# Mixer of a two-layer encoder: the Fourier and value projections as one seven-part product, with the mirrored half made by a permutation

## The chip, the core and the metric

The kernel runs on one core of one Trainium2 chip. The metric is the device time of one execution in microseconds (us), median over runs. In the text PE is the matrix engine (TensorE), DVE the vector engine, ACT the scalar engine, POOL GpSimd, and SP the engine that issues most of the transfers. PSUM, where products land, has eight banks; one 128x512 f32 block fills a bank.

## What is computed

Two layers on 512 tokens by 1024 channels. Each layer is a half-step SwiGLU feed-forward block (FFN), a mixer, and a second FFN:

```python
x = x + 0.5 * swiglu(rms_norm(x, ffn1_norm[l]), ffn1_w_in[l], ffn1_w_out[l])
x = x + mixer(rms_norm(x, mix_norm[l]), mix_w_in[l], ...)
x = x + 0.5 * swiglu(rms_norm(x, ffn2_norm[l]), ffn2_w_in[l], ffn2_w_out[l])

def mixer(h, w_in, gate_bias, rpb, w_na_out, w_f_out, w_o):
    z = h @ w_in                      # columns: q 512, k 512, v 512, u 512, two gates of 1024
    y_na = neighbourhood_attention(q, k, v, rpb) @ w_na_out     # 8 heads of 64
    y_f = fourier_mix(u) @ w_f_out    # real part of a 2-D DFT over positions and 128 channels, 4 groups
    g_na, g_f = sigmoid(ga + gate_bias[0]), sigmoid(gf + gate_bias[1])
    return (g_na * y_na + g_f * y_f) @ w_o
```

## The kernel before, in words

**Precision.** Each f32 operand is split into a rounded part and the rest (hi and lo: `split`, L296 to L302; one ACT copy, one DVE subtraction). A product is three matmuls: hi by hi, hi by lo, lo by hi (`mm3` L291, or `late_low` L449, which puts the products with the low half of the weights last). Every weight granule (128x1024 f32, 512 KB) is loaded by SP (L150), rounded by ACT into `whi` (L181) and subtracted by DVE into `wlo` (L184); with `dma=True` or a `plus` key, POOL issues a second transfer that adds another granule in memory (L152). `whi` and `wlo` have three buffers each, so a granule is prepared when the PE has done with the granule three earlier. `Stream` (L255) holds the granules in one fixed order, loads up to 8 ahead and prepares 2 ahead.

**Seven-part products.** The FFN blocks and the gates multiply a 2x2 block matrix in seven block products instead of eight (`ORDER`, `product` L458). A product is 24 matmuls of 512 columns: 4 blocks of 128 input channels, 2 blocks of 128 tokens, 3 matmuls. The left factors of products 4 to 7 are sums and differences of quarters of the activations (t1 to t4), made on DVE from f32 copies `raw` and then split (`combine`, L576, in the FFN); `snap` (L519, ACT) and `less` (L525, DVE) take results out of PSUM.

**Norm.** `quad(i, j)` (L359) transposes one quarter of x on the PE (8 transposes) and writes the split activations. Three quarters are done at the end of the FFN stage (L840, L841, L844) and the last, (1, 0), inside the next stage (`settle`). In the FFN an f32 copy `raw` is kept; in the mixer (`self.mix`) it is not, and each 128x256 piece is split straight out of PSUM (L374). `rstd` (L424) makes the inverse norms with twelve small DVE instructions (L310 to L315, L428, L429); `spread` (L441) sends them through memory into a row `R`, by two POOL transfers.

**Mixer before the change**, in program order (L1315 to L1350):

- `proj_U` (L982): u is wanted as the sum and the difference of token t and token 511-t, for t below 256. It multiplies the first 256 tokens (`straight`) and the last 256 in reversed order (`mirrored`, whose left factor `flip` is a reversed copy made by ACT and DVE, L993 and L994): 96 matmuls.
- `proj_V` (L1027): 96 matmuls. Its results are split into `v` straight out of PSUM.
- `bias_for(0)`: position biases; 68 KB gathers on SP (L1100) into `bw` (2 buffers), then six POOL additions (L1106) into `bm` (4 buffers).
- `four_pos` four times (the transform over positions), `proj_q(0)`, `proj_k(0)` (each 24 matmuls, `proj_T` L970), `four_ch` four times (over channels; each takes two banks, emptied by ACT at L1070 and DVE at L1072 to L1074), `proj_q(1)`.
- Attention by head pairs (L1342): `att_next(hp)` transposes the probabilities of the last pair and starts the scores of the next (four banks); `att_probs` (L1129) does softmax, with eight DVE and sixteen ACT instructions for one pair of heads; `att_outs` multiplies by v.

The instructions of each engine run in the order that a list scheduler gives them when the kernel is built; each engine takes them strictly in that order.

Of the kernel before, what the change touches and what calls it, by code (L numbers as in the profile page):

```python
# [17 lines left out]
P = 128  # L18
# [28 lines left out]
def _granules():  # L47
# [7 lines left out]
    for l in range(L):  # L55
        for w in (1, 2):
# [15 lines left out]
            if w == 1:  # L72
                s = (l, 0)
                for name, n in (("u", 4), ("v", 4), ("qk", 8), ("f", 4)):
                    for g in range(n):
                        put(s, name, g)
                for i in range(2):
                    for g in range(2):
                        put(s, "n", i, g)
                    for q in "acdb":  # L80
                        for g in range(2):
                            put(s, "g" + q, i, g)
                for q in "acdb":
                    for g in range(2):
                        put(s, "w" + q, 0, g)
# [7 lines left out]
def encoder_kernel(  # L93
# [95 lines left out]
    def stage_items():  # L189
# [4 lines left out]

        def strassen(s, name, idx, sizes, order, dma=False):
            def key(q, g):
# [6 lines left out]
            for m in order:  # L203
                for g in range(len(sizes)):
# [7 lines left out]
                    elif m == 4:  # L212
                        add(d2[g])
                    elif m == 5:
                        add(d)
                    elif m == 6:
                        add(d, a, then=b.key if dma else None)
                    else:
                        add(c)

        def out_sizes(c):
# [14 lines left out]
        for l in range(L):  # L236
# [3 lines left out]
            two = (1024, 1024)  # L240
            for name, n in (("u", 4), ("v", 4), ("qk", 8), ("f", 4)):
                for g in range(n):
                    add(Raw((s, name, g)))
            st += 1
# [73 lines left out]
    class Norm:  # L318
# [40 lines left out]
        def quad(self, i, j):  # L359
            self.tiles(i)  # L360
            js = slice(j * 256, (j + 1) * 256)
            hq, lq = self.h[i][:, :, js], self.l[i][:, :, js]
            if not self.mix:
                raw = self.raw[i, j] = slot(F32, "xr")
            for k2 in range(2):
# [5 lines left out]
                for k in range(2):  # L371
                    kt = 2 * k2 + k
                    if self.mix:
                        split(hq[:, kt, :], lq[:, kt, :], tr[:, k, :], self.gain(4 * i + kt))  # L374
                    else:
                        S.activation(raw[:, kt, :], tr[:, k, :], AF.Copy, scale=self.gain(4 * i + kt))
            if not self.mix:
                split(hq, lq, raw)

# [145 lines left out]
    def less(ps, t):  # L525
        for b in range(2):
            V.tensor_tensor(t[:, b, :], ps[b], t[:, b, :], ALU.subtract)  # L527

    def stage_ffn(norm, nxt, late):
# [26 lines left out]
        first = norm.idx == 0  # L556
        norm.tiles(1)
        t4 = (hx[0][:, :, 256:512], lx[0][:, :, 256:512])
# [14 lines left out]

        acts = {1: (hx[0], lx[0], 0), 2: (hx[1], lx[1], 0), 3: (hx[1], lx[1], 256), 4: (*t4, 0)}

        def combine(m):  # L576

            if m == 5:
                V.tensor_tensor(raw[0, 0], raw[0, 0], raw[0, 1], ALU.subtract)
                acts[5] = parts(raw[0, 0], "t1")  # L580
            elif m == 7:
                V.tensor_tensor(raw[0, 1], raw[0, 1], raw[1, 1], ALU.subtract)
                acts[7] = parts(raw[0, 1], "t3")
            elif m == 6:
                V.tensor_tensor(raw[0, 0], raw[1, 1], raw[0, 0], ALU.add)
                acts[6] = parts(raw[0, 0], "t2")
            else:
                V.tensor_tensor(raw[1, 0], raw[1, 0], raw[0, 0], ALU.subtract)
                split(*t4, raw[1, 0])

# [345 lines left out]
    def stage_mixer(l, norm, nxt):  # L936
# [4 lines left out]

        msk = mp.tile([P, 3, 256], F32, tag="msk", name=nm("msk"), bufs=1)
        ch = mp.tile([P, 2, 2, P], F32R, tag="ch", name=nm("ch"), bufs=1)
        R = mp.tile([P, T], F32, tag="R", name=nm("R"), bufs=1)
# [17 lines left out]

        def wide():

            wh, wl = ws.next()
            for k in range(2):
                c = slice(k * T, (k + 1) * T)
                yield wh[:, c], wl[:, c]

        def proj_T(scale):  # L970
            ps = bank()
            wh, wl = ws.next()
            for kt in range(DT):
                c = slice(kt * P, (kt + 1) * P)
                mm3(ps, wh[:, c], wl[:, c], *xs[kt], kt == 0, kt == DT - 1)
            t = tmp(s="q")
            V.tensor_tensor(t, ps, R, ALU.mult)
            hi, lo = hilo("q")
            split(hi, lo, t, scale)
            return hi, lo  # L980

        def proj_U():  # L982
            pss = [bank() for _ in range(4)]

            def straight(kt, wh, wl):
                for c in range(2):
                    lh, ll = [z[:, c * P : (c + 1) * P] for z in xs[kt]]
                    mm3(pss[c], lh, ll, wh, wl, kt == 0, kt == DT - 1)

            def mirrored(kt, wh, wl):  # L990
                flip = tmp(F32R, s="flip")
                xh, xl = [z.bitcast(F32) for z in xs[kt]]
                S.activation(flip[:, 0:256], xh[:, 511:255:-1], AF.Copy)  # L993
                V.tensor_copy(flip[:, 256:512], xl[:, 511:255:-1])  # L994
                for c in range(2):
                    lh, ll = [flip[:, z + c * P : z + c * P + P] for z in (0, 256)]
                    mm3(pss[2 + c], lh, ll, wh, wl, kt == 0, kt == DT - 1)

            for g in range(2):
                for k, w in enumerate(wide()):  # L1000
                    straight(2 * g + k, *w)
                    mirrored(2 * g + k, *w)
                if g == 0:
                    norm.settle()
            w = [*wide(), *wide()]
            for kt in range(4):
                mirrored(4 + kt, *w[kt])
            for kt in range(4):
                straight(4 + kt, *w[kt])
            norm.rstd()  # L1010
            norm.spread(R)
            constants()
            outs = []
            for c in range(2):
                t = tmp(s="uf")
                S.activation(t, pss[2 + c], AF.Copy, scale=norm.rflip[:, c : c + 1])
                both = []
                for op in (ALU.add, ALU.subtract):
                    w = tmp(s="ue")
                    V.scalar_tensor_tensor(w, pss[c], norm.r[:, c : c + 1], t, ALU.mult, op)  # L1020
                    hi, lo = hilo("u")
                    split(hi, lo, w)
                    both.append((hi, lo))
                outs.append(both)
            return outs

        def proj_V():  # L1027
            pss = [bank() for _ in range(4)]
            for g in range(4):
                for k, (wh, wl) in enumerate(wide()):  # L1030
                    kt = 2 * g + k
                    for c in range(4):
                        lh, ll = [z[:, c * P : (c + 1) * P] for z in xs[kt]]
                        mm3(pss[c], lh, ll, wh, wl, kt == 0, kt == DT - 1)
            outs = []
            for c in range(4):
                t = slot(F32R, "v", (2, T))
                split(t[:, 0, :], t[:, 1, :], pss[c], norm.r[:, c : c + 1])
                outs.append(t)
            return outs  # L1040

# [43 lines left out]
        def proj_q(hp):  # L1085
            q[hp] = proj_T(DH**-0.5)

        def proj_k(hp):
            k[hp] = proj_T(None)
            o.append(hilo("o"))  # L1090

# [94 lines left out]

        def att_outs(hp):
            for i in (2 * hp, 2 * hp + 1):
                att_out(i, pt_.pop(i))
# [124 lines left out]

        u = proj_U()  # L1315
        vt = proj_V()
        bias_for(0)
# [6 lines left out]
        vch = {i: (t[:, 0, :], t[:, 1, :]) for i, t in ((0, vt[0]), (1, vs[0]), (2, vt[1]), (3, vs[1]), (4, vt[2]), (5, vs[2]), (6, vt[3]))}  # L1324
        for g in range(4):
            four_pos(g)
        proj_q(0)
        proj_k(0)
        for g in range(4):
            four_ch(g)  # L1330
        proj_q(1)
        def f_rows():
# [8 lines left out]

        for hp in range(3):  # L1342
            att_next(hp)
            bias_for(hp + 1)
            proj_k(hp + 1)
            if hp:
                att_outs(hp - 1)
            if hp < 2:
                proj_q(hp + 2)
        f_some(2)  # L1350


# [18 lines left out]
        swap_pools(0)  # L1371
        f_some(2)
        next(first)
        att_outs(3)
        t12, _ = next(first)
        ws.prep(ws.pos + 2)
        f_some(1)
        bias = []
# [163 lines left out]
def _weights(g):  # L1542
    wst = np.zeros((len(GRAN), P, 1024), np.float32)
    for l in range(L):
# [27 lines left out]
        for i, z in enumerate(_qk_granules(wi)):  # L1572
            wst[GRAN_AT[s, "qk", i]] = z
        for name, m in (("u", u), ("v", v)):
            for i in range(4):
                wst[GRAN_AT[s, name, i]] = _wide(m, (2 * i, 2 * i + 1), 0)

        def four(name, i, w1, c1, w2, c2):
# [4 lines left out]

        wo = g["mix_w_o"][l]
        four("w", 0, wo, 0, wo, T)
        for i in range(2):
# [72 lines left out]
```

## Time and profile before

| | |
|---|---|
| median of 3 runs (lowest, highest) | 1907.44 us (1906.4, 1908.48) |
| the profiled execution, its own time | 1906.98 us |
| its span in the profile | 1905.2 us |
| PE busy | 1890.9 us (99%), 9189 matmuls and transposes |
| DVE, ACT, POOL busy | 1608.4 (84%), 1161.3 (61%), 199.0 us (10%) |
| first mixer, u begins / v begins / four_pos begins | about 336.4 / 359.2 / 381.0 us |
| second mixer, u begins | about 1281.4 us |

How to read it: a matmul's row shows how long it was in the array (389 ns for 512 columns), but the next one starts before it is through, so the distance between two starts is what one costs. A line of the timeline gives the start, the duration, the engine, the source line, the operation, what it writes and reads, its shape and how many such follow each other, and in brackets how long the engine was idle before it and what ended that.

### The profile page before, as it was taken

What the parts mean: (1) busy time and instruction counts of PE and PEld (TensorE: products, weight loads), DVE (VectorE), ACT (ScalarE), POOL (GpSimd) and SP (SyncE); (2) the same over time, 40 slices, a digit from 0 to 9 for tenths busy, and PEclk for the clock granted to TensorE, in tenths of its full rate; (3) what the DMA queues carried; (4) which work ended last, traced back from release to release, by engine and by line L of the source; (5) the groups of instructions that cost most, each with busy time, mean ns of one, the idle gap of its engine ahead of it and who ended that gap; (6) DMA issues with size and microseconds to landing.
All of it is one profiled execution on the core that took longest, in us unless ns stands there. A gap on an engine that the chain in (4) does not pass through costs nothing.

```text
span 1905.2 us, 25187 instructions
## 1 busy us (share of the span) xinstructions
PE 1890.9 (99%) x9189; PEld 1586.3 (83%) x9189; DVE 1608.4 (84%) x2000; ACT 1161.3 (61%) x1676; POOL 199.0 (10%) x246
## 2 busy tenths in 40 slices
PE   9999999999999999999999999999999999999998
PEld 7888888888888888888888888888888888888886
DVE  7877899586889987889997778995769899787898
ACT  6655665467566755566665556663675566555664
POOL 0101010310111011001010100103101101000010
PEclk9999999999999999999999999999999999999999
DMA  9777499323786777649877765974147867776594
GB/s 301 204 209 184 150 254 313 100 73 99 212 217 163 174 199 205 175 154 263 245 189 212 185 178 156 277 266 129 50 121 215 211 172 173 208 177 177 171 276 144
DMA packets 104924, 361.09 MB, mean 190 GB/s; under 512 B 12064, under 2 KB 14240, under 8 KB 104800
## 3 DMA queue, kind: packets, MB, share of 16 engines
q1 hardware_dynamic: 77856, 267.42, 40.4%
q0 software_dynamic: 26800, 92.04, 27.1%
q8 instruction: 72, 1.18, 0.3%
q14 instruction: 52, 0.43, 0.1%
q10 hardware_dynamic: 144, 0.02, 0.0%
HBM read 354.18 MB, written 2.11 MB: 187 GB/s over the span
## 4 chain that ended last, share of the span: by engine, by line
PE 95%; DVE 2%; DMA 1%; ACT 1%; issue 0%; SPq 0%; DVEq 0%; ACTq 0%
PE A L453 9%; PE A L454 9%; PE A L456 9%; PE o L454 7%; PE o L453 7%; PE o L456 7%; PE ps L292 5%; PE ps L293 5%; PE ps L294 5%; PE B L453 5%; PE B L454 5%; PE B L456 5%; PE C L454 2%; PE C L453 2%; PE C L456 2%; PE tr L545 2%
## 5 line engine op out<-in xcount | busy, mean ns | idle before, releaser
L181 ACT ACTIVATE whi<-raw 128x1024 fp32r<-128x1024 f32 (+1 forms) x528 | 546.3, 1037 | 416.9 <-PE A L454 119.2
L184 DVE TENSOR_TENSOR wlo<-raw,whi 128x1024 fp32r<-128x1024 f32 (+1 forms) x528 | 630.1, 1198 | 187.3 <-ACT whi L181 185.2
L152 POOL DMA_DIRECT2D raw<-in_wst_dram x158 | 136.1, 871 | 1283.1 <-DMA raw<-in_wst_dram 631.1
L166 DVE TENSOR_TENSOR raw<-raw,raw 128x1024 f32<-128x1024 f32 (+1 forms) x146 | 172.2, 1189 | 1.2
L454 PE MATMUL A<-whi,xl 128*128 128x512 f32 x384 | 149.5, 389 | 0.0
L453 PE MATMUL A<-whi,xh 128*128 128x512 f32 x384 | 149.4, 389 | 0.0
L456 PE MATMUL A<-wlo,xh 128*128 128x512 f32 x384 | 110.5, 389 | 0.0
L176 ACT ACTIVATE whi<-raw 128x1024 fp32r<-128x1024 f32 (+1 forms) x79 | 81.8, 1035 | 36.2 <-PE A L454 9.6
L177 DVE SCALAR_TENSOR_TENSOR wlo<-raw,whi 128x1024 fp32r<-128x1024 f32 (+1 forms) x79 | 93.2, 1191 | 10.7 <-ACT whi L176 10.6
L638 ACT ACTIVATE th<-sn,rh 128x512 f32<-128x512 f32 x80 | 56.7, 714 | 69.5 <-DVE sn L527 69.5
L522 ACT ACTIVATE sn<-A 128x512 f32<-128x512 f32 x96 | 56.5, 589 | 53.5 <-PE A L456 53.5
L456 PEld LDWEIGHTS A<-wlo,xh 128*128 128x128 f32 x384 | 72.1, 188 | 15.0
L454 PEld LDWEIGHTS A<-whi,xl 128*128 128x128 f32 x384 | 72.1, 188 | 14.8
L453 PEld LDWEIGHTS A<-whi,xh 128*128 128x128 f32 x384 | 72.1, 188 | 14.8
L453 PE MATMUL B<-whi,t1h 128*128 128x512 f32 x192 | 76.2, 397 | 0.0
L453 PE MATMUL A<-whi,t3h 128*128 128x512 f32 x192 | 75.2, 392 | 0.0
L453 PE MATMUL C<-whi,xh 128*128 128x512 f32 x192 | 74.9, 390 | 0.0
L453 PE MATMUL A<-whi,t2h 128*128 128x512 f32 x192 | 74.9, 390 | 0.0
L454 PE MATMUL B<-whi,t1l 128*128 128x512 f32 x192 | 74.8, 390 | 0.0
L454 PE MATMUL A<-whi,t3l 128*128 128x512 f32 x192 | 74.8, 390 | 0.0
L454 PE MATMUL C<-whi,xl 128*128 128x512 f32 x192 | 74.7, 389 | 0.0
L454 PE MATMUL A<-whi,t2l 128*128 128x512 f32 x192 | 74.7, 389 | 0.0
(410 smaller groups left out, 4784.6 us busy)
## 6 DMA issues: line engine op xcount, KB each, us to landing
raw<-in_wst_dram SPq DMA_DIRECT2D x466, 512.0 KB
raw<-in_wst_dram POOLq DMA_DIRECT2D x162, 512.0 KB, 7.8
raw<-in_wst_dram SPq DMA_DIRECT2D x30, 256.0 KB
vs<-v SPq DMA_DIRECT2D x12, 256.0 KB
bw<-in_rpb_dram SPq DMA_DIRECT2D x32, 68.0 KB
x<-in_xin_dram SPq DMA_DIRECT2D x4, 512.0 KB
raw<-in_wst_dram POOLq DMA_DIRECT2D x8, 256.0 KB, 8.2
dft<-in_dft_dram POOLq DMA_DIRECT2D x8, 256.0 KB, 6.2
```

The source lines that it names most:

```text
L152: G.dma_start(out=self.t, in_=wst[GRAN_AT[self.plus]][:, 0 : self.n], accum_op=ALU.add)
L166: V.tensor_tensor(self.raw.t, self.raw.t, self.add.t, ALU.add)
L176: S.activation(hi, t, AF.Copy, scale=-1.0)
L177: self.last = V.scalar_tensor_tensor(lo, t, -1.0, hi.bitcast(F32), ALU.mult, ALU.subtract)
L181: S.activation(hi[:, cs], t[:, cs], AF.Copy)
L184: self.last = V.tensor_tensor(lo[:, cs], t[:, cs], hi[:, cs].bitcast(F32), ALU.subtract)
L292: PE.matmul(ps, lh, rh, start=start, stop=False, skip_group_check=again)
L293: PE.matmul(ps, lh, rl, start=False, stop=False, skip_group_check=again)
L294: PE.matmul(ps, ll, rh, start=False, stop=stop, skip_group_check=again)
L453: PE.matmul(ps, lh, rh, start=start, stop=False, skip_group_check=again)
L454: PE.matmul(ps, ll, rh, start=False, stop=False, skip_group_check=again)
L456: PE.matmul(ps, lh, rl, start=False, stop=stop, skip_group_check=again)
```

## The change

The diff, cut to its core; lines are those of the file before.

```diff
-                for name, n in (("u", 4), ("v", 4), ("qk", 8), ("f", 4)):
+                for q in "abcd":
+                    for g in range(2):
+                        put(s, "u" + q, 0, g)
+                for name, n in (("qk", 8), ("f", 4)):
...
+            qk = [(s, "qk", g) for g in range(8)]
+            strassen(s, lambda q: "u" + q, 0, two, (1, 5, 6, 2, 7, 3, 4), behind={5: qk[0:1], 6: qk[1:2], 2: qk[2:3]})
...
-            if not self.mix:
-                raw = self.raw[i, j] = slot(F32, "xr")
+            raw = self.raw[i, j] = slot(F32, "xr")
...
-                    if self.mix:
-                        split(hq[:, kt, :], lq[:, kt, :], tr[:, k, :], self.gain(4 * i + kt))
-                    else:
-                        S.activation(raw[:, kt, :], tr[:, k, :], AF.Copy, scale=self.gain(4 * i + kt))
-            if not self.mix:
-                split(hq, lq, raw)
+                    S.activation(raw[:, kt, :], tr[:, k, :], AF.Copy, scale=self.gain(4 * i + kt))
+            split(hq, lq, raw)
...
-        def proj_U():
...
-        def proj_V():
...
+        def proj_UV():
+            acts, combine = combos(norm, None)
+            pa = pair("A")
+            product(pa, acts[1], K4, True)
+            combine(5)
+            s1 = snap(pa)
+            pb = pair("B")
+            product(pb, acts[5], K4, True)
+            norm.settle()
+            norm.rstd()
+            norm.spread(R)
+            combine(6)
+            sb = snap(pb)
+            q0 = proj_T(DH**-0.5)
+            product(pa, acts[6], K4, False, again=True)
+            s2 = snap(pa)
+            combine(7)
+            k0 = proj_T(None)
+            pc = pair("C")
+            product(pc, acts[2], K4, True)
+            with tc.issue_after(less(pc, s1).ins):
+                q[0] = q0()
+            q1 = proj_T(DH**-0.5)
+            combine(4)
+            with tc.issue_after(ws.items[ws.prepped - 1].last.ins):
+                k[0] = k0()
+            product(pa, acts[7], K4, False, again=True)
+            less(pa, sb)
+            q[1] = q1()
+            constants()
+            product(pb, acts[3], K4, False, again=True)
+            less(pb, s2)
+            split(uh, ul, s2)
...
+            product(pa, acts[4], K4, False, again=True)
+            S.activation(mir, mirror, AF.Copy)
             for c in range(2):
+                pm = bank()
+                PE.matmul(pm, mir, uh[:, 1 - c, :], start=True, stop=False)
+                PE.matmul(pm, mir, ul[:, 1 - c, :], start=False, stop=True)
...
-        for g in range(4):
-            four_pos(g)
-        proj_q(0)
-        proj_k(0)
-        for g in range(4):
-            four_ch(g)
-        proj_q(1)
...
+        proj_k(1)
+        for g in range(4):
+            four_pos(g)
+        proj_q(2)
+        att_next(0)
+        bias_for(1)
+        for g in range(4):
+            four_ch(g)
+        proj_k(2)
+        proj_q(3)
+        att_next(1)
+        bias_for(2)
+        att_outs(0)
+        proj_k(3)
+        f_some(1)
+        att_next(2)
+        bias_for(3)
+        f_some(2)
+        att_outs(1)
+        f_some(1)
```

- u and v become the two column halves of one 2x2 block product in seven parts, 168 matmuls. The weights come in four granule pairs a to d, two of them summed in memory by POOL.
- The mixer's norm keeps `raw` as the FFN's does; `combos` is the FFN's `combine` made common, with a fourth pair of buffers for t4.
- Three projections by channels (q0, k0, q1; `proj_T` now returns a function that takes the result out of PSUM later) stand between the parts.
- The mirrored half of u is made after the product: 4 matmuls with a 128x128 reversal matrix `mir`.
- k1, then `four_pos`, q2, the first scores (`att_next(0)`), then `four_ch`, then k2 and q3. Before, `four_pos`, q0, k0, `four_ch`, q1 and only then the first scores.

## The prediction

> **What bounds the kernel now.** I read the busy times of the page first, then the chain of waits, then the granted clock.
>
> ```profile
> PE 1890.9 (99%) x9189; PEld 1586.3 (83%) x9189; DVE 1608.4 (84%) x2000; ACT 1161.3 (61%) x1676; POOL 199.0 (10%) x246
> ...
> PEclk9999999999999999999999999999999999999999
> ...
> PE 95%; DVE 2%; DMA 1%; ACT 1%; issue 0%; SPq 0%; DVEq 0%; ACTq 0%
> ```
>
> PE is busy for 99% of the span, the chain that ended last is 95% PE, and the clock is at its top in every slice. So each matmul removed is worth its spacing, and each microsecond in which PE waits is lost in full. The spacing comes from the timeline of PE:
>
> ```profile
> 353.63 0.39 PE L292 MATMUL ps<-whi,xh 128*128 128x512 f32 x1
> 353.86 0.39 PE L293 MATMUL ps<-wlo,xh 128*128 128x512 f32 x1
> 354.09 0.39 PE L294 MATMUL ps<-whi,xl 128*128 128x512 f32 x1
> ```
>
> Starts lie 0.23 us apart (0.2268 over longer stretches; 0.12 for 256 columns, 0.11 for a transpose). Summing all distances between starts beyond these leaves PE idle for only about 10 us in the whole run, 1.26 us in one place at most, so little can be won except work. Next, which engine has room beside PE: the windows of the FFN's end, of u and of v.
>
> ```profile
> core 0: us, PE busy (x) PEld busy (x) DVE busy (x) ACT busy (x) POOL busy (x), PEclk, DMA share, GB/s
> ...
> 300.00:336.00 36.00, 36.00 (x169) 30.04 (x168) 35.95 (x44) 21.84 (x34) 0.55 (x1) 1.00 0.84 299
> 336.00:359.00 23.00, 23.00 (x107) 19.14 (x106) 11.75 (x34) 9.05 (x19) 8.29 (x14) 1.00 0.20 56
> ```
>
> DVE is full (35.95 of 36 us) up to the moment when u begins at 336.4, and half free (11.75 of 23) behind it. u's start asks DVE for little; a seven-part product asks for sums and differences just there.
>
> **The change, part by part, per layer.**
>
> *Removed work.* u and v were 192 matmuls of 512 columns; now 7 x 24 = 168, and 4 for the mirror: 20 x 0.2268 = −4.5 us. The projections q0, k0, q1 and the others are moved, not added. The reversed copies `flip` go too (DVE and ACT, beside PE: nothing).
>
> *The start of the mixer.* The norm's three quarters at the FFN's end now have an f32 copy and a split of 128x1024; before, they were split in 128x256 pieces. DVE's work there shrinks a little (three subtractions of 1.14 for twelve of 0.42: 1.6 us less of 36), too little to unload it. The chain that counts begins where the x additions end:
>
> ```profile
> 327.91 2.35 DVE L184 TENSOR_TENSOR wlo<-raw,whi 128x1024 fp32r<-128x1024 f32 x2
> ...
> 336.57 1.28 DVE L664 SCALAR_TENSOR_TENSOR x<-o,x 128x512 f32<-128x512 f32 x2
> ```
>
> Two subtractions of 128x1024 go in 2.35 and the next starts 2.27 after the first: 1.14 each. x is ready at 337.8. In the order that the changed program is built with, DVE then makes `wlo`, `xl` of quarter (0,1) and the t1 difference: 337.8 + 3 x 1.14 = 341.3, and ACT's t1h (a copy of 128x1024, 1.05) ends at 342.4. PE has product 1 (24 x 0.2268 = 5.4) until 341.85: it waits about 0.6. Product 5 and eight transposes end at about 348.9. Meanwhile DVE has t1l, an addition of granules, `wlo`, another addition, `wlo`, `xl` of (1,0) and the t2 sum, six after t1l at 1.14, and some 0.6 us of the inverse norms: t2 at 351.2, t2h at 352.3. PE waits 3.4. t2l stands behind a `wlo`: 0.95 more. With 0.1 at t3 the start waits 5.0 us. From both sides: the FFN's start has the same sums, and PE lost only 0.35 us in that stretch (626 to 690), but there other pieces of work stand between its products: 0.4 is the lower end. The upper is 8: the accumulating transfers of granules b and a land 7.5 to 10 us after POOL issues them, and POOL issues the second behind a transfer that waits for DVE:
>
> ```profile
> 327.15 0.55 POOL L947 DMA_DIRECT2D ch<-in_chan_dram  x1 [30.02 <-DVE wlo L184]
> ```
>
> *POOL's additions.* `bias_for(0)` now runs in POOL's order right behind the first two accumulating transfers, so at about 330 to 342, beside the chain above instead of at 355:
>
> ```profile
> 355.26 5.13 POOL L1106 TENSOR_TENSOR bm<-bw,msk 128x256 f32<-128x256 f32 x6
> ...
> 357.65 2.18 DVE L184 TENSOR_TENSOR wlo<-raw,whi 128x1024 fp32r<-128x1024 f32 x1 [6.93 <-ACT whi L181]
> 360.42 1.23 DVE L184 TENSOR_TENSOR wlo<-raw,whi 128x1024 fp32r<-128x1024 f32 x1 [0.52 <-ACT whi L181]
> ```
>
> The subtraction that meets them takes 2.18 instead of 1.23: +0.95 (in the second layer 2.60, +1.4). Three batches, of which at least one meets a link of the chain: I take 1.0, range 0 (they fall elsewhere) to 2.5.
>
> *Middle.* k0 and q1 stand between parts 6, 2 and 7, and cover t3 and t4; SP takes the bias gathers ahead of weight loads and POOL the row `R` behind `bm`, but `R` lands about 370 and is used first at 376: nothing, up to 0.5 if that cover fails. u's halves end on DVE just before the transform over positions: 0.2 (0 to 1).
>
> *The transform over channels.* Now it follows the scores of pair 0, and k2 follows it. Call the start of those scores S. The scores (16 x 0.12) and `four_ch` (24 x 0.12) end at S + 4.9. By then scores hold four banks and `four_ch` has gone through all eight; k2 takes the bank of the first `four_ch` that `fq` (ACT, L1070) empties. ACT takes instructions in order, and `fq` stands behind the sixteen of pair 0's softmax. Its length before:
>
> ```profile
> 409.23 0.41 DVE L1138 CUSTOM_DVE_ANT_0 s<-ps,bm 128x256 f32<-128x256 f32 x1
> ...
> 409.75 0.51 ACT L1144 ACTIVATE s<-s,nmx 128x256 f32<-128x256 f32 x1 [2.04 <-DVE nmx L1138]
> ...
> 415.31 1.70 ACT L1151 ACTIVATE s<-s,rs 128x256 f32<-128x256 f32 x4
> 416.91 0.62 ACT L298 ACTIVATE q<-q 128x512 fp32r<-128x512 f32 x1
> ```
>
> From DVE's first score instruction to ACT's next work: 416.91 − 409.23 = 7.7. When does that first one start? DVE must first do two of v's halves (1.2), the sixteen instructions behind `four_pos` (4 x 1.95, from L1055 to L1057: 0.60 + 0.60 + 2 x 0.37), four subtractions (2.4), a `wlo` (1.15) and q2's exit (0.6): 13.2 us, begun about 10 us ahead of S. So S + 3 without a wait, S + 4.5 with the 1.5 us that DVE would wait for ACT and for q2; I take 4.5, since q2's exit can't come before S. Two subtractions stand behind the first score instruction, which holds the second exponential by 1.0. So `fq` ends at S + 4.5 + 7.7 + 1.0 + 0.4 = S + 13.6, and PE waits 13.6 − 4.9 = 8.7 us. Lower end 4.5 (DVE free), upper 10. Before, `four_ch` came ahead of the scores and its `fq` had nothing such in front of it; nothing hides this one, for no PE work stands behind k2 that could pass it.
>
> *Sum.* −4.5 + 5.0 + 1.0 + 0.2 + 8.7 = +10.4 per layer; both layers have the same order: +20.8. The profiled execution took 1906.98 us (its span of 1905.2 and 1.78 around it), 0.46 under the median: 1906.98 + 20.8 = **1927.8**.
>
> **Rivals.**
>
> *All waits are hidden*: only the removed work counts, 1906.98 − 2 x 4.54 = 1897.9. For it: PE hardly ever waits now, with the same seven-part product in the FFN. Against: DVE's 35.95 of 36 us, and ACT's strict order at `fq`. It decides the other way as soon as the waits are under 4.5 us per layer. Chance 0.06.
>
> *Only the start waits* (k2's bank is free in time): −4.5 + 6.0 + 0.2 + 0.6 for small waits = 2.3, x 2: 1911.6. Chance 0.10.
>
> *Only k2 waits* (the start is covered as in the FFN): −4.5 + 0.4 + 0.2 + 8.7 = 4.8, x 2: 1916.6. For it: DVE gets slack if granules are prepared earlier than I count. Chance 0.17.
>
> *The clock falls in the gaps.* Before there is no long gap, so the trace has only the start of the run:
>
> ```profile
> 2.73 3.59 PE L138 MATMUL ps<-warm 128*128 128x512 bf16 x9 [2.73 <-ACT warm L135]
> ```
>
> From 2.73 to 6.39, where the spacing reaches 0.23, PE does ten matmuls in 3.66 us instead of 2.27: 1.4 lost. If the t2 gap and the k2 gap each cost that again: 4 x 1.4 = 5.6 more, 1933.4. Chance 0.17, since only the k2 gap is surely long. The Trainium skill, "TensorE: Matmul & The Clock Gate", section "HAM oscillation — how this bites in real kernels", says that an idle stretch over about 3.4 us halves PE's clock until it has been busy about as long again; the slow 3.66 us at the start agree, and that it also happens in mid-run no gap here is long enough to show.
>
> *No change that can be measured*: a measurement of this kernel can tell about 0.2%, so 1903.2 to 1910.8; waits of about 4.5 per layer. Chance 0.04.
>
> **How the numbers follow.** Forecast 0.46, clock 0.17, only k2 0.17, only start 0.10, faster 0.06, no change 0.04. The range takes the first three: from 1915 (below only k2, 1916.6) to 1937 (the clock case and some 4 us of the upper ends). All lower ends together would give +0.4 per layer (1907.8), all upper ends +17 (1941); I don't expect all of one side at once. Faster by over 0.2% 0.06, within 0.04, slower 0.90.
>
> **What would show it.** PE gaps in front of the matmuls with t1h (0.6), t2h (3 to 4) and t2l (1) behind u's start, ended by ACT and DVE; POOL's `bm` additions at 330 to 342 with a stretched DVE instruction beside them; in front of k2 the largest gap, 7 to 10 us, ended by `fq`; 9158 matmuls or somewhat fewer in the records; PEclk under 9 in slices with the gaps if the clock falls. Wrong is the start's step if t2h comes before product 5's end; wrong is k2's if ACT does `fq` ahead of the softmax or if PE finds another bank.

## The result and the profile after

The changed kernel takes 1951.84 us (median of 6 runs, 1949.83 to 1954.48) against 1907.69 for the kernel before: a ratio of 1.0233, 95% interval 1.0219 to 1.0246. It is 44.2 us slower, where 20.8 were forecast; the sign was right, the size was under half of it. The time also lies above the 1941 that the prediction gave for all upper ends together, and above the 1946.6 that this makes with the 5.6 us of its clock rival. The profiled execution has a span of 1949.7 us, 44.5 more than before.

The page of the changed kernel, the same three views as in the prediction:

```profile
PE 1902.7 (98%) x9149; PEld 1591.2 (82%) x9149; DVE 1657.3 (85%) x2010; ACT 1190.2 (61%) x1704; POOL 217.1 (11%) x254
...
PEclk9999999889999999999999999999899999999999
...
PE 82%; DVE 7%; ACT 5%; issue 3%; DMA 2%; SPq 0%; POOL 0%; DVEq 0%; ACTq 0%; POOLq 0%
```

PE has 40 matmuls fewer, as computed, and yet more busy time: matmuls that run at a lower clock are longer. The granted clock falls to 8 tenths in two slices in the first layer's mixer and in one in the second's, and of the chain that ended last, which was 95% PE, 17% now are DVE, ACT, DMA and "issue". What PE waited for in all (total, number of times, longest), from the waits of PE:

```profile
PE A L454 <- ACT t2h L304: 9.8, 2, 5.1
PE ps L298 <- ACT fq L1088: 7.5, 2, 3.8
PE B L454 <- ACT t1h L304: 6.6, 2, 4.7
...
PE ps L298 <- DVE q L988: 3.4, 2, 1.7
...
PE ps L298 <- DVE nmx L1155: 2.6, 2, 1.3
PE A L454 <- ACT sn L523: 2.0, 2, 1.2
```

Each pair is one per layer. t1h, t2h and fq are three of the four waits that the prediction named (the fourth, t2l, is shorter). The windows of the first layer, around t1h, t2h, the scores with `four_ch`, and k2, show the second thing:

```profile
core 0: us, PE busy (x) PEld busy (x) DVE busy (x) ACT busy (x) POOL busy (x), PEclk, DMA share, GB/s
...
336.00:349.00 13.00, 11.03 (x46) 8.96 (x45) 13.00 (x14) 9.43 (x17) 11.09 (x10) 0.87 0.56 128
349.00:363.00 14.00, 9.23 (x32) 6.72 (x32) 13.19 (x21) 6.91 (x9) 3.64 (x3) 0.76 0.88 239
421.00:435.00 14.00, 7.62 (x52) 6.20 (x50) 9.92 (x33) 9.61 (x28) 4.02 (x6) 0.71 0.11 21
435.00:446.00 11.00, 10.58 (x36) 8.55 (x37) 8.01 (x22) 5.40 (x11) 0.00 (x0) 0.75 0.07 14
```

The third column from the end is the granted clock: 0.87, 0.76, 0.71 and 0.75, where it was 1.00 before. DVE is busy for 13.00 of 13 and 13.19 of 14 us around t1 and t2.

To divide the 44.5 us I took the distance from each matmul's start to the next and subtracted the usual spacing (0.227, 0.12 for 256 columns). An excess over 0.3 us (for the shorter matmuls, over 1.3 times the spacing) counts as a wait, the rest, mostly spacings of 0.43 for 0.227, as lower clock. The bound between the two is a choice; it can move a few tenths of a us from one to the other:

| part | first layer | second layer | forecast per layer |
|---|---|---|---|
| 20 matmuls less | −4.5 | −4.5 | −4.5 |
| start: waits for t1h, t2h, t2l | 8.7 | 12.7 | 6.0 (chain 5.0, POOL 1.0) |
| start: lower clock behind them | 2.5 | 3.3 | 0 (a rival) |
| scores to k2: waits | 8.8 | 8.8 | 8.7 |
| scores to k2: lower clock | 2.9 | 2.9 | 0 (a rival) |
| elsewhere, as the remainder (the gates' `snap` above all) | 3.0 in both | | 0.2 |

**The scores to k2** went as the prediction had it, almost to the tenth. The rows of PE, DVE and ACT in the timeline of the first layer:

```profile
421.73 1.69 PE L1141 MATMUL ps<-q,q 64*128 64x256 f32 x24
...
426.49 0.38 PE L298 MATMUL ps<-b,ch 128*128 128x256 f32 x1 [1.71 <-DVE q L988]
428.47 0.55 PE L298 MATMUL ps<-b,ch 128*128 128x258 f32 x1 [1.31 <-DVE nmx L1155]
435.42 0.80 PE L298 MATMUL ps<-xh,whi 128*128 128x512 f32 x1 [3.77 <-ACT fq L1088]
436.01 0.63 PE L299 MATMUL ps<-xl,whi 128*128 128x512 f32 x1
436.44 0.63 PE L300 MATMUL ps<-xh,wlo 128*128 128x512 f32 x1
436.87 0.63 PE L298 MATMUL ps<-xh,whi 128*128 128x512 f32 x1
```

```profile
426.36 0.41 DVE L1155 CUSTOM_DVE_ANT_0 s<-ps,bm 128x256 f32<-128x256 f32 x1
```

```profile
433.42 1.69 ACT L1168 ACTIVATE s<-s,rs 128x256 f32<-128x256 f32 x4
435.01 0.62 ACT L1088 ACTIVATE fq<-ps 128x255 f32<-128x255 f32 x2
```

S is 421.73. The first score instruction on DVE starts at S + 4.6 (forecast 4.5), the first `fq` at S + 13.3, right behind the last normalisation, and k2 at S + 13.7 (forecast 13.6). Only the form differs: it is three waits, not one, since `four_ch` itself also wants banks that DVE must empty first, q2's and one of the scores'. Behind the last of them the matmuls start 0.43 us apart (the last three rows of PE).

**The start** went otherwise. DVE around t1 in the changed kernel:

```profile
341.89 0.67 DVE L429 TENSOR_TENSOR ms<-ssq 128x4 f32<-128x4 f32 x1
342.49 1.21 DVE L543 TENSOR_TENSOR xr<-xr,xr 128x1024 f32<-128x1024 f32 x1
343.63 0.66 DVE L430 TENSOR_SCALAR ms<-ms 128x4 f32<-128x4 f32 x1
...
347.72 1.81 DVE L169 TENSOR_TENSOR raw<-raw,raw 128x1024 f32<-128x1024 f32 x1
```

An instruction on 128x4 values keeps DVE for 0.60 us (341.89 to 342.49), where such a one costs 0.08 elsewhere (352.90 to 352.98). POOL works on `bm` beside it:

```profile
341.00 4.99 POOL L1123 TENSOR_TENSOR bm<-bw,msk 128x256 f32<-128x256 f32 x3 [1.91 <-DMA bw<-in_rpb_dram]
```

A layer has 24 of these additions, six for each pair of heads. POOL does twelve of them between 331 and 352, so the six from 341.00 on, beside the inverse norms, are already those of `bias_for(1)`. The prediction counted only those of `bias_for(0)` there.

In the second layer ACT stands still as well:

```profile
1306.31 1.06 ACT L184 ACTIVATE whi<-raw 128x1024 fp32r<-128x1024 f32 x1 [4.27 <-DMA raw<-in_wst_dram]
1307.27 1.03 ACT L304 ACTIVATE xh<-xr 128x1024 fp32r<-128x1024 f32 x1
```

It waits 4.27 us for a granule that is summed in memory, and the split for the norm and t1h stand behind that in ACT's order.

### The profile page after: what moved, and what is told of

Read it like the earlier page. It is cut to its first block, busy times and chain, and to the rows that moved or that the text cites. A ratio compares the mean times of both kernels' runs of the same rounds, so it can differ in the third digit from the quotient of the medians.

```text
span 1949.7 us, 25182 instructions
## 1 busy us (share of the span) xinstructions
PE 1902.7 (98%) x9149; PEld 1591.2 (82%) x9149; DVE 1657.3 (85%) x2010; ACT 1190.2 (61%) x1704; POOL 217.1 (11%) x254
## 4 chain that ended last, share of the span: by engine, by line
PE 82%; DVE 7%; ACT 5%; issue 3%; DMA 2%; SPq 0%; POOL 0%; DVEq 0%; ACTq 0%; POOLq 0%
PE A L455 9%; PE A L454 9%; PE A L457 9%; PE o L457 6%; PE o L454 6%; PE o L455 6%; PE B L454 5%; PE B L455 5%; PE B L457 4%; PE C L455 2%; PE C L454 2%; PE C L457 2%; DMA raw<-in_wst_dram 2%; DVE wlo L187 2%; PE tr L576 2%
## 5 line engine op out<-in xcount | busy, mean ns | idle before, releaser
L184 ACT ACTIVATE whi<-raw 128x1024 fp32r<-128x1024 f32 (+1 forms) x536 | 554.6, 1038 | 444.7 <-PE A L455 136.7
L155 POOL DMA_DIRECT2D raw<-in_wst_dram x166 | 143.3, 878 | 1279.2 <-DMA raw<-in_wst_dram 816.6
L169 DVE TENSOR_TENSOR raw<-raw,raw 128x1024 f32<-128x1024 f32 (+1 forms) x154 | 182.6, 1193 | 1.2
L179 ACT ACTIVATE whi<-raw 128x1024 fp32r<-128x1024 f32 (+1 forms) x83 | 86.1, 1037 | 45.5 <-PE A L455 12.6
L180 DVE SCALAR_TENSOR_TENSOR wlo<-raw,whi 128x1024 fp32r<-128x1024 f32 (+1 forms) x83 | 99.6, 1211 | 15.7 <-ACT whi L179 14.4
L454 PE MATMUL A<-whi,t2h 128*128 128x512 f32 x208 | 83.0, 401 | 9.8 <-ACT t2h L304 9.8
L454 PE MATMUL B<-whi,t1h 128*128 128x512 f32 x208 | 83.9, 405 | 6.6 <-ACT t1h L304 6.6
L455 PE MATMUL A<-whi,t2l 128*128 128x512 f32 x208 | 82.8, 400 | 0.7 <-DVE t2l L305 0.6
L454 PE MATMUL A<-whi,t3h 128*128 128x512 f32 x208 | 81.5, 392 | 2.0 <-ACT sn L523 2.0
L455 PE MATMUL B<-whi,t1l 128*128 128x512 f32 x208 | 82.2, 397 | 0.0
L455 PE MATMUL C<-whi,xl 128*128 128x512 f32 x208 | 81.0, 389 | 0.0
```

The source lines that it names most:

```text
L155: G.dma_start(out=self.t, in_=wst[GRAN_AT[self.plus]][:, 0 : self.n], accum_op=ALU.add)
L169: V.tensor_tensor(self.raw.t, self.raw.t, self.add.t, ALU.add)
L179: S.activation(hi, t, AF.Copy, scale=-1.0)
L180: self.last = V.scalar_tensor_tensor(lo, t, -1.0, hi.bitcast(F32), ALU.mult, ALU.subtract)
L184: S.activation(hi[:, cs], t[:, cs], AF.Copy)
L454: PE.matmul(ps, lh, rh, start=start, stop=False, skip_group_check=again)
```

## The experiments

**1. POOL's additions later.** `spread` is POOL's transfer of the row R; the additions are queued behind it, and those of `bias_for(1)` behind them.

```diff
-        u, vt = proj_UV()
-        bias_for(0)
+        u, vt, spread = proj_UV()
+        with tc.issue_after(spread.ins):
+            bias_for(0)
```

> The changed kernel with POOL's additions of bias_for(0) held until POOL has issued the transfer of the row R; all else as in the change. In the trace of the changed kernel the small DVE instructions of the inverse norms (128x4) take 0.66 us while POOL adds and 0.15 behind it, and three subtractions of 128x1024 take 1.74 to 1.83 instead of 1.21. Theory A (POOL's additions stretch the chain that t1 and t2 wait for): three times 0.55, seven times 0.5 and one time 0.6, so DVE gets about 5 to 6 us back by the time of t2 in the first layer and as much or more in the second; the waits for t1h and t2h fall from 8.7 (first layer) and 12.7 us (second) to 3 to 5 and 4 to 7, and with some of the slow matmuls behind them gone the time falls from 1951.8 to 1934 to 1941. Theory B (DVE's queue is too long by itself and POOL only happens to run beside it): under 4 us in all, 1948 to 1952. The gap in front of k2 stays in both.

Measured: 1947.0 us (1945.36 to 1947.38), 4.8 less. That lies just above theory B's price and under A's. The mechanism of A is there; the same small instruction of DVE, and the addition that took 1.81:

```profile
344.26 0.16 DVE L317 TENSOR_SCALAR r<-rt 128x4 int32<-128x4 int32 x1
344.33 1.22 DVE L169 TENSOR_TENSOR raw<-raw,raw 128x1024 f32<-128x1024 f32 x1
```

They are back at 0.07 (344.26 to 344.33) and 1.22. In the first layer the waits fell to 1.1 (t1h), 3.2 (t2h) and 0.8 (t2l): 5.1, which is the 5.0 that the prediction counted without POOL. So POOL's additions cost 3.6 us of waits there, not 1.0. In the second layer t2h fell from 5.3 to 3.1, but t1h rose from 4.8 to 5.6: what holds it is not POOL's additions. That is where most of the expected gain went.

**2. `four_ch` ahead of the scores.**

```diff
-        att_next(0)
-        bias_for(1)
+        proj_k(2)
         for g in range(4):
             four_ch(g)
-        proj_k(2)
+        att_next(0)
+        bias_for(1)
         proj_q(3)
```

> The changed kernel with k2 and then four_ch ahead of the first scores; u and v stay one product. Theory A (fq behind the softmax on ACT costs the 8.4 us of waits between the scores and k2, and the slow matmuls behind them 2.9): 23.3 us are lost there in both layers; most of it goes: 1929 to 1933, less a little if four_ch now waits for the subtractions behind four_pos. Theory B (banks and ACT are late anyway since the whole mixer is behind): the gap moves to another place and the time falls by under 6 us, over 1945.

Measured: 1944.54 us (1942.66 to 1945.95), 7.3 less, not 20, and between the two theories. The wait for `fq` is gone, but another has come; from the waits of PE:

```profile
PE ps L1177 <- ACT s L1168: 5.0, 4, 1.9
```

The transposes of the first pair's probabilities wait for its softmax. In the kernel before, k1 and q2 (10.9 us) stand between these scores and the transposes; here only q3 (5.4) is left, since q0, k0 and q1 have been used up at the start and k1, q2 around `four_pos`. Summed from the scores to the transposes, waits and lower clock go from 23.3 us (both layers) to about 16. Theory A had the price of the wait and forgot what then stands next.

**3. Both.** The two edits together.

> Both edits of the two runs before. If the two waits are independent, the gains add: 1951.8 less about 14 and 20, 1914 to 1921. If PE then only waits at the next late thing (DVE is behind by the same work), the sum is smaller: 1925 to 1935. The start wait that is left by the counting of the prediction (5.0 per layer, without POOL) would leave 1907 - 9 + 10 = 1908 as the lower end.

Measured: 1939.61 us (1937.68 to 1943.46), 12.2 less; 4.8 and 7.3 are 12.1. The gains add within the spread of the runs, so the two places are independent as far as these can tell, but each is smaller than was expected of it, and the sum misses both ranges.

**4. Only `four_ch` behind the scores, with the old u and v.**

```diff
-        for g in range(4):
-            four_ch(g)
         proj_q(1)
...
             att_next(hp)
             bias_for(hp + 1)
+            if hp == 0:
+                for g in range(4):
+                    four_ch(g)
```

> The kernel before, with u and v as they were, and only four_ch moved behind the first scores (q1 ahead of the scores, k1 behind four_ch, as k2 is in the change). Theory A: fq behind sixteen softmax instructions, 11.5 to 12 us behind the start of the scores, k1 ready at 4.9: 6.6 to 7.1 us of waits and some 2.5 us of slow matmuls per layer, so 1907.7 + 18 to 20 = 1925 to 1928, range 1921 to 1932. Theory B (the wait belongs to the DVE backlog that the new u and v leave): under 3 us per layer, 1908 to 1914.

Measured: 1923.57 us (1923.39 to 1924.42), ratio 1.0081 (1.0066 to 1.0096), 16.1 more than the kernel before. Theory A, a little under its middle. PE in front of k1:

```profile
414.73 0.80 PE L292 MATMUL ps<-xh,whi 128*128 128x512 f32 x1 [4.29 <-ACT fq L1070]
```

The same wait, ended by the same `fq`, in a kernel that has nothing else of the change. The stretch costs 9.2 and 8.6 us per layer, 0.6 in the kernel before; 2.8 and 2.3 of it are matmuls at the lower clock. So this order of work costs about 16 us by itself, and more with the new u and v (23.3), where PE also waits for banks that DVE has yet to empty (the first two of the three waits above).

**5. The transfer of `ch` later too.** `ch` (128x512 constants) was the first transfer of the mixer in POOL's order; here it is issued with the other constants, behind R.

```diff
-        G.dma_start(out=ch, in_=chan)
         nc.sync.dma_start(out=msk, in_=mask)
...
         def constants():
+            tc.keep_in_program_order(G.dma_start(out=ch, in_=chan))
```

> The run with the additions of bias_for(0) held, and beside that the transfer of the constants ch, which stands first in POOL's order of the mixer, put behind R. In the second layer of that run ACT stands still for 5.0 us until a granule of product 5 that POOL adds up in memory has landed, and t1h stands behind it on ACT; POOL issued that transfer at 1292.5, right behind ch, which had waited 33 us for DVE. Theory A (ch holds POOL's queue, and the granule itself is long there): the transfers start many us sooner, the wait for t1h falls from 5.6 to 0.5 to 1.5 in the second layer and stays about 1 in the first, and with the slow matmuls behind it 1947.0 becomes 1938 to 1942. Theory B (the transfers are late because the memory is busy or the granule lands late): 1945 to 1948.

Measured: 1937.66 us (1936.69 to 1938.15), 9.3 less than run 1: theory A, just under its range. POOL in the second layer, first in run 1, then here:

```profile
1291.96 0.56 POOL L963 DMA_DIRECT2D ch<-in_chan_dram  x1 [33.05 <-DVE wlo L187]
1292.51 1.78 POOL L155 DMA_DIRECT2D raw<-in_wst_dram  x2
```

```profile
1280.00 0.85 POOL L155 DMA_DIRECT2D raw<-in_wst_dram  x1 [23.48 <-PE o L457]
1281.29 0.86 POOL L155 DMA_DIRECT2D raw<-in_wst_dram  x1 [0.43 <-DVE wlo L187]
```

`ch` waits 33 us until DVE is through with the FFN's granules, and the accumulating transfers of product 5's weights, queued behind it, go out at 1292.5; they landed 10.6 and 14.0 us later. Without `ch` in front they go at 1280.0 and 1281.3 and land after 5.6 and 7.7. t1h's wait falls from 5.6 to 0.54 us, and both layers now start alike: 0.5 + 3.2 + 0.5 to 0.8, again close to the 5.0 of the count.

**6. `four_ch` ahead of the scores, with q1 and k1 behind `four_pos`.** On top of run 5, only q0 and k0 stay between the parts of the product. The diff is cut to its core; q3 and the fillers `f_some` behind it move too.

```diff
-            q1 = proj_T(DH**-0.5)
...
-        proj_k(1)
         for g in range(4):
             four_pos(g)
-        proj_q(2)
-        att_next(0)
-        bias_for(1)
+        proj_q(1)
+        proj_k(1)
         for g in range(4):
             four_ch(g)
+        att_next(0)
+        bias_for(1)
+        proj_q(2)
         proj_k(2)
```

> As the run with ch put late, and only q0 and k0 stand between the parts of the product; q1 and k1 follow four_pos, then four_ch, then the first scores, and two projections cover each softmax as in the kernel before. Theory A (what is lost between four_pos and the second scores is only the cover that q1 and k1 gave): the 23.3 us that the changed kernel loses there go nearly all, and do not come back at the transposes: 1940 less 23 is 1917, range 1911 to 1922. Theory B (v and u end so late on DVE that this stretch waits in any order, and t3 and t4 lack the cover of q1): 1926 or more.

Measured: 1929.07 us (1924.36 to 1930.87), 8.6 less than run 5, not 23. From the waits of PE:

```profile
PE A L454 <- ACT t2h L304: 6.1, 2, 3.1
PE ps L298 <- ACT u L304: 4.9, 2, 2.4
```

The waits of k2 for `fq` and at the transposes are gone (0.5 us per layer is left in front of the scores), but `four_pos` now waits 2.4 us per layer for u, which k1 had covered. The edit took a cover away that I had not counted. By its number this is theory B, and the late u is what B named; "in any order" does not hold, since run 9 covers that wait. Theory A was right about the place of the loss, not about the sum.

**7. Product 2 between 1 and 5.** On top of run 6:

```diff
-            strassen(s, lambda q: "u" + q, 0, two, (1, 5, 6, 2, 7, 3, 4), behind={5: qk[0:1], 6: qk[1:2]})
+            strassen(s, lambda q: "u" + q, 0, two, (1, 2, 5, 6, 7, 3, 4), behind={5: qk[0:1], 6: qk[1:2]})
```

with the calls in `proj_UV` in the same order and the quarter (1, 0), `settle`, ahead of t1.

> As the run before, with product 2 between 1 and 5, so that PE has 5.4 us more before it wants t1 and again before t2; it needs the quarter (1, 0), which is transposed when the last x is ready. Theory A (the start waits for a chain of DVE and ACT instructions of fixed length): t1h and t2h are ready in time, and about 1 to 2 us of wait for the new quarter take the place of 4 to 5 of wait and 1.5 of slow matmuls per layer: 6 to 9 us less than the run before, 1904 to 1912. Theory B (DVE has 36 of 36 us of work and nothing is gained by another order): within 2 us of the run before.

Measured: 1930.5 us (1928.92 to 1934.55): theory B by its number. t1h and t2h were in time, but PE waited 3.7 us for the split quarter (1, 0), which product 2 needs, and 1.3 to 1.5 for a granule later. Without the granule's wait the start cost 5.3 and 5.6 us with the lower clock, against 5.9 and 7.0 in run 6.

**8. The clock.** Behind the last product of the kernel before, bursts of 40 matmuls (bf16, 512 columns) on zeros with waits between them; they add to its work, so its time is of no use, and it was executed once.

```diff
...
+        for n in (0, 1, 2, 3, 4, 5, 6, 7, 8, 10, 12, 16, 8, 7, 6, 5, 4, 3, 2, 1):
+            for _ in range(n):
+                S.activation(gap, pw, AF.Copy, scale=0.0)
+            for _ in range(40):
+                PE.matmul(pw, gap[:, 0:P], gap, start=True, stop=True)
```

> The kernel before, and behind its last product twenty bursts of 40 matmuls of 512 columns on zeros, with chains of 0 to 16 copies by ACT between them, so that PE waits between about 0.5 and 9 us before each burst; the time of the whole is of no use, only the spacing inside the bursts. Theory A (as the changed kernel's trace has it, where a wait of 2.1 us was followed by spacings of 0.43): waits over a bound between 1.3 and 1.9 us slow the matmuls behind them to 0.43 for 3 to 4 us, which loses 1.4 to 2 us each time whatever the length. Theory B (only waits over 3.4 us do it): bursts behind 2 and 3 us keep 0.22.

Measured: PE waited 0.75, 1.38, 2.01, 2.64, 3.26 us and so on up to 10.2; in front of the first burst, where no chain stands, it waited 6.3. A burst at full rate takes 8.43 us (spacing 0.216). Windows of three bursts, behind waits of 2.6, 3.3 and 2.0 us, each from the burst's first start; the third column from the end is the granted clock:

```profile
1947.22:1955.60 8.38, 8.38 (x39) 3.82 (x40) 0.00 (x0) 0.00 (x0) 0.00 (x0) 1.00 0.00 0
1959.28:1967.70 8.42, 8.42 (x32) 3.47 (x33) 0.00 (x0) 0.00 (x0) 0.00 (x0) 0.80 0.01 2
...
2146.09:2156.20 10.11, 10.11 (x39) 4.26 (x40) 0.00 (x0) 0.00 (x0) 0.00 (x0) 0.83 0.01 2
```

All twelve bursts behind 3.26 us or more had 6 to 14 matmuls at 0.43 and lost 1.3 to 2.9 us, whatever the wait's length. None behind 0.75, 1.38 or 2.64 did. Of the two behind 2.01, one did (the last row), and there the lower clock began inside the burst. So neither theory is right as put: 3.3 us was always enough here, and 2.0 can be. The Trainium skill, "TensorE: Matmul & The Clock Gate", section "HAM oscillation — how this bites in real kernels", gives about 3.4 us of idling as the bound. The bound measured here is lower: one wait of 2.01, the first t1h wait of the changed kernel (1.97 us), behind which the matmuls run at 0.43 at once, and the waits of 2.4 us for u in run 6 brought the lower clock too.

Why 2.01 can do what 2.64 does not is seen in the clock of the traces: it changes in steps of 3.41 us. In all traces here each stretch of half clock inside the run lasts 3.41 us or a multiple of it, and within a trace they all begin whole multiples of 3.41 us apart. Counted back from such a beginning, the wait of 2.64 (the first two rows) is divided over two steps, and that of 2.01 (the last two) lies in one:

```profile
1942.34:1945.76 3.42, 2.24 (x11) 0.80 (x9) 0.00 (x0) 1.05 (x2) 0.00 (x0) 1.00 0.00 0
1945.76:1949.17 3.41, 1.95 (x10) 0.89 (x10) 0.00 (x0) 1.34 (x3) 0.00 (x0) 1.00 0.00 0
...
2143.73:2147.14 3.41, 1.40 (x7) 0.51 (x6) 0.00 (x0) 1.79 (x3) 0.00 (x0) 1.00 0.00 0
2147.14:2150.56 3.42, 3.42 (x9) 1.22 (x8) 0.00 (x0) 0.00 (x0) 0.00 (x0) 0.50 0.00 0
```

PE is idle for 1.18 and 1.46 us of the first two steps and for 2.01 of the third, behind which the clock is at half. Over all the traces, start and end aside, 44 of 44 steps at full clock with 1.93 us or more of idle PE were followed by half clock, and 7 of 24 with 1.2 to 1.92. So what counts is how much of a wait falls into one step, and for waits from about 2 us to twice that it is a matter of chance, more likely for the longer ones.

**9. Each wait covered.** On top of run 6: q0 ahead of product 6 on PE (`last[-1]` is q0's last matmul), q1 ahead of `four_pos`, k1 and q2 behind it.

```diff
             q0 = proj_T(DH**-0.5)
-            product(pa, acts[6], K4, False, again=True)
+            with tc.issue_after(last[-1].ins):
+                product(pa, acts[6], K4, False, again=True)
...
+        proj_q(1)
         for g in range(4):
             four_pos(g)
-        proj_q(1)
         proj_k(1)
+        proj_q(2)
...
         bias_for(1)
-        proj_q(2)
         proj_k(2)
+        proj_q(3)
```

> As the run with everything late (q0 and k0 between the parts, four_ch ahead of the scores, bm and ch late), with two moves: q0 stands ahead of product 6 on PE instead of behind its first matmuls, since it needs only the quarter (1, 0), which is split 2.2 us before t2h is ready; and q1 stands ahead of four_pos, which waited 2.6 us for u, so that k1 and q2 follow four_pos. Theory A (each wait is the cover that is missing just there): the wait for t2h of 3.2 falls to about 1, t2l's 0.5 goes, four_pos waits 0, and most of the slow matmuls behind these go; the start costs 2 to 3 us per layer instead of 6, the stretch before four_pos 0.5 instead of 4.4; the gates keep their 2.4: 1929 less 14 to 18, 1911 to 1915, slower than the kernel before by no more than 0.4%. Theory B (each wait that is closed opens as large a one behind it, since DVE and ACT are behind): 1920 or more.

Measured: 1923.59 us (1921.28 to 1923.94), outside A's range and theory B by its number. One long wait was left:

```profile
PE ps L434 <- DVE r L321: 11.3, 2, 5.7
```

A matmul of two columns, which reverses the inverse norms r, stood in front of q0 on PE; r is ready only when its small instructions have passed between large ones on DVE. Beside it the start kept 0.4 us in front of t1h, and `four_pos` and the attention were covered.

**10. That matmul behind product 7.** `flip` is the matmul and its copy, taken out of `rstd`.

```diff
+            end7 = product(pa, acts[7], K4, False, again=True)
             less(pa, sb)
+            with tc.issue_after(end7.ins):
+                norm.flip()
```

> As the run with each wait covered, in which PE stood 5.8 us per layer in front of a matmul of two columns that reverses r (ready only when the twelve small instructions of the inverse norms have passed between large ones on DVE), with q0 behind it; here that matmul stands behind product 7. Theory A (each wait is the cover that is missing just there): the start costs 2 us per layer (t1h 0.5, the split of the quarter (1, 0) about 1, some slow spacing) instead of 9: 1923.6 less 13 to 15, 1908 to 1911. Theory B (the next late thing is as late): 1918 or more.

Measured: 1906.23 us (1904.4 to 1910.12, 11 runs) against 1907.11, ratio 0.9997 (0.9988 to 1.0006): theory A, a little better than expected. The start costs 0.7 us in each layer, and the granted clock is at its top in every slice of the page. This is 45.6 us under the changed kernel with the same arithmetic, and level with the kernel before. The 9.1 us of saved work are not seen, since what PE loses between its matmuls over the whole run sums to 20.2 us against 10.0: the profiled execution divides it among some ten places of 0.3 to 1.4 us, the gates' `snap` (1.4 and 1.3) first.

**11. t1, the quarter (1, 0) and t2 ahead of the granules.** `combine(5)`, `settle` and `combine(6)` of run 10 with a higher priority.

> As the run before, and the difference t1, the quarter (1, 0) and the sum t2 get ahead of the preparation of granules in DVE's and ACT's order. Theory A: t1h and q0 are ready when PE is; 0.5 us per layer is left at the start. What PE then waits for over the whole run is 16 to 18 us against 10 in the kernel before, and 9.1 us of work are saved: 1904 to 1908, level with the kernel before or just under it. Theory B (what is put back on DVE, the granules, is waited for instead, and nothing is gained): within 1 us of the run before or above it.

Measured: 1910.45 us (1907.79 to 1912.03), ratio 1.0013 (1.0005 to 1.0022): theory B. t1h's 0.5 us went, and a wait of 1.0 for a granule's `wlo` in q0 came in each layer.

## Why the prediction was right or wrong

- **Removed work**, −4.5 per layer: right, by the count of matmuls. (The 9158 that the prediction expected in the records does not follow from its own 20 per layer; 9189 less 40 is the 9149 of the page.)
- **The chain of the start**, 5.0 per layer: right as a chain; run 1 shows 5.1 (first layer) and run 5 4.3 and 4.5 of waits once the two disturbances are taken away.
- **POOL's additions**, 1.0 with an upper end of 2.5: the place was right, the size was not. I priced one stretched subtraction of 128x1024, the row that I had. Small instructions of the inverse norms stand on the chain as well, and six of them were held by 0.5 us or more each, all six beside the additions of `bias_for(1)`, which I had not counted there at all. Run 1 puts it at 3.6 us of waits in the first layer.
- **The landing of summed granules** was named only for the upper end, with `ch` in front of it on POOL. In the second layer it was the wait for t1h: run 5 moves `ch` and 5.1 us go.
- **`four_ch` behind the scores**, 8.7: right, with its chain confirmed at each step and by run 4 in the old kernel. That the 8.8 agrees to 0.1 is partly luck: the scores are 24 matmuls in 1.6 us, not 16 times 0.12, and the 8.8 holds 1.3 us of small waits beside the three of 7.5.
- **The clock**: this is the step of the sum that failed most. The likeliest case priced each wait at its length, so the lower clock stood in the sum at nothing, and was kept as a rival at 0.17, with 1.4 us in two places per layer, because only the k2 gap was surely long. It falls behind all the long waits, t1h's of 1.97 us too, and costs 5.4 and 6.2 us per layer, 11.6 in all. Run 8 shows 1.3 to 2.9 per wait.
- **Rivals**: "all waits are hidden", "only the start" and "only k2" fall with the profile after; the rival that came nearest was the clock's, 1933.4.

The forecast of +20.8 lacks 23.7 of the profiled 44.5 us: 11.6 for the clock, 9.4 at the start's waits (21.4 instead of 12), and about 3 elsewhere. What remains argued only is the division of the last 3 us; the gates' `snap` waits behind a granule on ACT, and no run took that apart.

## What to carry to other kernels

Where PE is saturated, work that covers a wait is a stock of its own: moving three projections to one place takes their cover from three others, and in five of these runs (1, 2, 3, 6 and 9) a gain came out at about a third of what was expected, because another wait stood behind or took its place. Price a wait of PE at its length and, where it leaves PE idle for about 2 us in one step of the clock, at some 1.3 to 2.9 us more. Read each engine's order at the entry of a stage, queue by queue: a transfer that must wait (here `ch`), a small matmul that needs a late value (here r) or a chain on ACT (here the softmax) delays all that is queued behind it, however early that would be ready.

## What the runs showed of the hardware

Waits of PE of 3.3 us or more were always followed by 6 to 14 matmuls at 0.43 us instead of 0.216, and one of two waits of 2.0 us was too (run 8). The clock changed only in steps of 3.41 us, and a step with 1.93 us or more of idle PE was followed by one at half clock in 44 of 44 cases.

While POOL adds 128x256 blocks, a DVE instruction on 128x4 values held in SBUF keeps DVE for 0.60 us instead of 0.07, and one on 128x1024 can take 1.81 instead of 1.22. The Trainium skill, "SBUF — State Buffer", section "Who interferes with whom", says that a DVE instruction with two SBUF inputs contends with a POOL instruction that reads SBUF, and that this contention is an exclusive lock. The additions agree with that: a loss of about 0.5 to 0.6 us that does not depend on the DVE instruction's size, and is near the 0.69 us of one POOL addition (2.08 for three, at 331.34 in the changed kernel). `TENSOR_SCALAR` on one input was held as well (343.63, 0.66 us). POOL is held too: the three additions at 341.00 take 4.99 us.
